# A mixture turned on the vector engine instead of on TensorE, in a transformer block on one Trainium2 core

## The chip, the cores and the metric

One Trainium2 chip, one core of it. The metric is the device time of one execution in microseconds (us); three executions of the kernel before were timed, and one more was profiled. All arrays are 32-bit floats.

## The reference: what is computed

A block for 256 tokens of width 2048: a norm modulated by a conditioning vector, one wide input product, two mixers (gated linear attention "gla", block attention "moba"), a gated mixture of their two up-projections, an output product with a residual, and a feed-forward part. What matters here is the mixture:

```python
y_gla = o_gla @ w_up_gla[l]
y_moba = o_moba @ w_up_moba[l]
g_gla, g_moba = jnp.split(jax.nn.sigmoid(gates), 2, axis=-1)
x = x + gt1[:, None] * ((g_gla * y_gla + g_moba * y_moba) @ w_out[l])
```

## The kernel before

TensorE (PE) multiplies in a reduced 32-bit format; for accuracy each operand is split into a high and a low half, and each product is three matmuls: high by high (L308), high by low weights (L309), low by high (L310). Two token groups m = 0, 1 of 128 tokens have a PSUM tile of 128 x 512 each.

Weights stream in tiles of 128 x 1024 (512 KB, two slices of the inner dimension), made by `w_tiles` (L113 on). SyncE (SP) issues the transfer into a buffer of the pool `rawp` (ten buffers), ScalarE (ACT) casts the high half `whi` (L124), VectorE (DVE) subtracts for the low half `wlo` (L125); these two have high priority and five buffers each (`hlp`). One tile feeds one step of twelve matmuls. So DVE can be up to some four tiles ahead of PE.

In the background a conditioning product runs beside this: its weights `araw` share `rawp`, and DVE accumulates them (L159, the first of a group L161); `background(per)` emits `per` such pieces a step. When a group is done, PE sums it across partitions (L184), ACT copies the row (L187), PE turns it (L190) and DVE adds three small results (L197 to L199).

The output of the mixture is needed with the model dimension on the partitions, for the product with `w_out`, while the up-projections deliver it with the tokens there. So it is turned. `up_moba(j)` forms one column block of 512 of the moba product and multiplies it by its gate (L647). `up_gla(j)` does so for the other branch (L653), adds both (L654), and `to_T` turns the sum: eight PE transposes of 128 x 128 (L638) into two PSUM tiles, then the high half by ACT (L243) and the low half by DVE (L244).

The order around it is: up_moba(0), up_moba(1), two gate products (blocks 16 and 17 of the input product, `in_block`), up_moba(2), up_gla(0), up_gla(1), up_gla(2), gate products 18 and 19, up_moba(3), up_gla(3), then `w_out` in column blocks (`block_tok` called for each). An up-projection has 4 tiles (48 matmuls), a gate product and a block of `w_out` 8. The programmer writes this order; a scheduler then places the instructions of each engine by priority, readiness and free buffers, and each engine runs its own list strictly in order.

Of the kernel before, what the change touches and what calls it, by code (L numbers as in the profile page):

```python
# [8 lines left out]
F32 = mybir.dt.float32  # L9
F32R = mybir.dt.float32r  # L10
# [4 lines left out]
ALU = mybir.AluOpType  # L15
AX = mybir.AxisListType

P = 128
# [3 lines left out]
W = 512  # L22
# [18 lines left out]
def block_kernel(ctx, tc, x, c, ada_w, ada_b, norm1_g, w_in, gate_w2, gate_b, gla_norm_g,  # L41
                 w_up_gla, w_up_moba, w_out, norm2_g, w_ffn_in, w_ffn_out, final_g, out):
    nc = tc.nc
# [7 lines left out]
    rawp = ctx.enter_context(tc.tile_pool(name="rawp", bufs=NRAW))  # L51
# [5 lines left out]
    def slot(name, dt=F32):  # L57
        return slots.tile([P, W], dt, name=name, tag="slot")

    def mm_ps():  # L60
        return mmp.tile([P, W], F32, name="mm", tag="mm")

    def ax_ps():
        return axp.tile([P, W], F32, name="ax", tag="ax")

    tt = nc.vector.tensor_tensor
# [8 lines left out]
    for j in (0, 2):  # L75
        for m in range(2):
            t = rawp.tile([P, 2, W], F32, name="x", tag="raw")
# [15 lines left out]
    for r0, v in ((0, ada_b[0, 0:2 * D]), (32, norm1_g[0]), (48, ada_b[0, 3 * D:5 * D]), (80, norm2_g[0]), (96, gate_b[0])):  # L93
        v = v.rearrange("(k p) -> k p", p=P)
# [19 lines left out]
    def w_tiles(w_ap, k0, k1, c0, ncols=W):  # L114

        wv = w_ap.rearrange("(k p) n -> p k n", p=P)
        step = 2 * W // ncols
        for k in range(k0, k1, step):
            n = min(step, k1 - k)
            raw, hi, lo = (pool.tile([P, 2 * W], dt, name=name, tag=tag)[:, 0:n * ncols] for pool, dt, name, tag in  # L120
                           ((rawp, F32, "raw", "raw"), (hlp, F32R, "whi", "hi"), (hlp, F32R, "wlo", "lo")))
            nc.sync.dma_start(raw.rearrange("p (k n) -> p k n", n=ncols), wv[:, k:k + n, c0:c0 + ncols])
            with tc.high_priority(offset=HP):
                nc.scalar.copy(hi, raw)  # L124
                tt(lo, raw, hi.bitcast(F32), ALU.subtract)  # L125
            yield k, [(hi[:, q * ncols:(q + 1) * ncols], lo[:, q * ncols:(q + 1) * ncols]) for q in range(n)]
# [98 lines left out]
    def background(n):  # L225
        owed[0] += n
        while owed[0] >= 1 and bg:
            owed[0] -= 1
            try:
                next(bg[0])  # L230
            except StopIteration:
                bg.pop(0)
                owed[0] += 1
        if not bg:
            owed[0] = 0.0
# [6 lines left out]
    def split_T(ps, hi, lo):  # L242
        nc.scalar.copy(hi, ps)  # L243
        tt(lo, ps, hi.bitcast(F32), ALU.subtract)  # L244
# [57 lines left out]
    def prod_tok(ps, m, hi, lo, wt, k0, first, last):  # L302

        for q, (wh, wl) in enumerate(wt):
            k = k0 + q
            xh, xl = kx(hi, k, m), kx(lo, k, m)
            f, l = first and q == 0, last and q == len(wt) - 1
            mm(ps, lhsT=xh, rhs=wh, start=f, stop=False)  # L308
            mm(ps, lhsT=xh, rhs=wl, start=False, stop=False)  # L309
            mm(ps, lhsT=xl, rhs=wh, start=False, stop=l)  # L310
# [10 lines left out]
    res = [[None, None] for _ in blocks]  # L321
# [286 lines left out]


    owed_T = []  # L610

    def block_tok(hi, lo, w_ap, nk, c0, per=0, ncols=W, lag=0):

        ps = [mm_ps(), mm_ps()]
        out = [t[:, 0:ncols] for t in ps]
        behind = []
        for k, g in w_tiles(w_ap, 0, nk, c0, ncols):
            behind.append((k, g))
            prod_tok(out[0], 0, hi, lo, g, k, k == 0, k + len(g) == nk)
            if len(behind) > lag:  # L620
                k1, g1 = behind.pop(0)
                prod_tok(out[1], 1, hi, lo, g1, k1, k1 == 0, k1 + len(g1) == nk)
            background(per)
            if owed_T and k > 0:
                to_T(*owed_T.pop())
        for k1, g1 in behind:
            prod_tok(out[1], 1, hi, lo, g1, k1, k1 == 0, k1 + len(g1) == nk)
        return out

    mx_h, mx_l = [None] * 8, [None] * 8  # L630

    def to_T(src, hi, lo, kp0):

        for i in range(2):
            ps = ax_ps()
            for q in range(2):
                for m in range(2):
                    nc.tensor.transpose(ps[:, q * T + m * P:q * T + (m + 1) * P],  # L638
                                        src[m][:, (2 * i + q) * P:(2 * i + q + 1) * P], ident)
            hi[kp0 + i], lo[kp0 + i] = slot("th", F32R), slot("tl", F32R)  # L640
            split_T(ps, hi[kp0 + i], lo[kp0 + i])

    def up_moba(j):
        ps = block_tok(om_h, om_l, w_up_moba, 8, j * W, pace[0])
        for m in range(2):
            g = res[13 + 2 * j][m]
            tt(g, ps[m], g, ALU.mult)  # L647

    def up_gla(j):
        ps = block_tok(og_h, og_l, w_up_gla, 8, j * W, pace[0])  # L650
        for m in range(2):
            g, y = res[12 + 2 * j][m], res[13 + 2 * j][m]
            tt(g, ps[m], g, ALU.mult)  # L653
            tt(g, g, y, ALU.add)  # L654
        to_T(res[12 + 2 * j], mx_h, mx_l, 2 * j)

    pace[0] = PACES[3]
    up_moba(0)
    up_moba(1)
    for bi in (16, 17):  # L660
        in_block(bi, 0, KT)()
    up_moba(2)
    up_gla(0)
    up_gla(1)
    up_gla(2)
    for bi in (18, 19):
        in_block(bi, 0, KT)()
# [62 lines left out]
    for j in range(4):  # L730
# [3 lines left out]
        if j < 3:  # L734
            ps = block_tok(mx_h, mx_l, w_out, KT, j * W, pace[0])
            while gt1[j] is None:
                background(1)
            for m in range(2):
                resid(m, j, 0, W, ps[m], gt1, j)
                for i in range(2):  # L740
                    norm2_T(j, i, m)
        else:
            while bg:
                background(1)
            preload_sqrt()
            ps = block_tok(mx_h, mx_l, w_out, KT, j * W, 0, 256)
            for m in range(2):
                resid(m, j, 0, 256, ps[m], gt1, 3)
                norm_part(m)
                norm2_T(j, 0, m)  # L750
            ps = block_tok(mx_h, mx_l, w_out, KT, j * W + 256, 0, 256, lag=KT)
            with tc.high_priority(offset=HP2):
                for m in range(2):
                    resid(m, j, 256, 256, ps[m], gt1, 4)
                    norm2_T(j, 1, m)
                    norm2_rstd(m)
                    if m == 0:
                        norm2(0, range(0, SPL))
                norm2(0, range(SPL, 8))
                norm2(1, range(8))  # L760
# [4 lines left out]
    for half, pairs in enumerate((range(0, 6), range(6, 11))):  # L765
        ac_h, ac_l = [None] * (2 * len(pairs)), [None] * (2 * len(pairs))
        for jj, j in enumerate(pairs):
# [4 lines left out]
            for m in range(2):  # L772
                t = slot("sa")
# [8 lines left out]
        if half == 1:  # L782
            for j in range(4):
                t = slot("fg")
# [4 lines left out]
        for j in range(4):  # L789
# [14 lines left out]
            with tc.high_priority(offset=HP2):  # L804
                for m in range(2):
# [3 lines left out]
                    for i in (2, 0, 1, 3):  # L809
                        t = x1[m][i]  # L810
# [32 lines left out]
```

## Time and profile before

| | us |
|---|---|
| median of three executions | 1460.25 |
| lowest, highest | 1459.01, 1460.31 |
| the profiled execution | 1460.44 |
| its span, first to last instruction | 1458.7 |
| PE busy in the span | 1434.1 |
| DVE busy | 1033.9 |
| ACT busy | 701.9 |

A row of the profile groups instructions by line, engine, operation and tiles, written out<-in. Matmuls overlap, so their durations add up to more than the busy time; the distance between starts tells what one costs. A wait is named after what ended last before the waiting instruction began. The granted clock is given as a share of the full one.

### The profile page before, as it was taken

How to read it: one execution, taken by the hardware profiler on the slowest of the kernel's cores; microseconds unless marked ns; L12 is line 12 of the kernel's file. 1: busy time of each engine (PE TensorE's matmuls, PEld its weight loads, DVE VectorE, ACT ScalarE, POOL GpSimd, SP SyncE). 2: the span in 40 equal slices, each digit the busy share in tenths (PEclk: the TensorE clock that was granted, in tenths of full speed). 3: DMA queues.
4: the chain of work that ended last, by engine and by line, in shares of the span. 5: the costliest groups of instructions: out<-in, count | busy, mean ns of one | idle time of the engine just before them, and what ended most of it. 6: DMA issues, size and time to landing. Idle time of an engine off the chain costs nothing.

```text
span 1458.7 us, 18395 instructions
## 1 busy us (share of the span) xinstructions
PE 1434.1 (98%) x6776; PEld 1178.4 (81%) x6776; DVE 1033.9 (71%) x1203; ACT 701.9 (48%) x936; POOL 8.6 (1%) x26
## 2 busy tenths in 40 slices
PE   6999999999999999999999999999999999999997
PEld 3788787888788878888888888888888888888887
DVE  4899988987799989888686676545555445555554
ACT  5745444644558534445654444444333444444443
POOL 0000000000000000000000000000000000000000
PEclk9999999999999999999999999999999999999999
DMA  9989999995636999999497888655566665556541
GB/s 333 362 305 367 337 323 308 316 317 184 199 114 205 371 335 336 328 324 369 147 322 267 268 282 288 193 182 188 195 194 192 197 188 188 188 187 224 189 150 59
DMA packets 191867, 365.49 MB, mean 251 GB/s; under 512 B 13848, under 2 KB 31484, under 8 KB 191776
## 3 DMA queue, kind: packets, MB, share of 16 engines
q1 hardware_dynamic: 189440, 360.56, 73.3%
q10 hardware_dynamic: 2336, 3.75, 0.8%
q8 instruction: 53, 0.87, 0.2%
q14 instruction: 38, 0.31, 0.1%
HBM read 362.16 MB, written 2.10 MB: 250 GB/s over the span
## 4 chain that ended last, share of the span: by engine, by line
PE 94%; DVE 2%; DMA 2%; ACT 1%; issue 1%; SPq 0%; DVEq 0%; ACTq 0%
PE mm L310 29%; PE mm L309 29%; PE mm L308 29%; DVE wlo L125 1%; DMA araw<-in_ada_w_dram 1%; PE ax L638 1%; PE ax L455 1%; DMA x<-in_x_dram 1%; DVE acc L159 0%; DMA w<-in_gla_gate_w_dram 0%; PE ax L184 0%; PE ax L276 0%; PE ax L690 0%; PE ax L334 0%; PE ax L153 0%
## 5 line engine op out<-in xcount | busy, mean ns | idle before, releaser
L125 DVE TENSOR_TENSOR wlo<-raw,whi 128x1024 fp32r<-128x1024 f32 x488 | 594.2, 1222 | 330.6 <-ACT whi L124 328.8
L124 ACT CAST whi<-raw 128x1024 fp32r<-128x1024 f32 x488 | 512.4, 1053 | 635.1 <-PE mm L310 367.2
L308 PE MATMUL mm<-whi,h2h 128*128 128x512 f32 x704 | 275.1, 391 | 1.0 <-ACT h2h L727 0.9
L310 PE MATMUL mm<-whi,h2l 128*128 128x512 f32 x704 | 274.2, 390 | 0.3 <-DVE h2l L728 0.3
L309 PE MATMUL mm<-wlo,h2h 128*128 128x512 f32 x704 | 274.0, 389 | 0.0
L309 PE MATMUL mm<-wlo,hTh 128*128 128x512 f32 x640 | 251.9, 394 | 0.4 <-DVE wlo L125 0.3
L308 PE MATMUL mm<-whi,hTh 128*128 128x512 f32 x640 | 250.3, 396 | 1.4 <-ACT hTh L296 1.3
L310 PE MATMUL mm<-whi,hTl 128*128 128x512 f32 x640 | 250.3, 393 | 0.5 <-DVE hTl L298 0.5
L159 DVE SCALAR_TENSOR_TENSOR acc<-araw,cs,acc 128x1024 f32<-128x1024 f32 (+1 forms) x184 | 227.4, 1236 | 26.7 <-DMA araw<-in_ada_w_dram 25.9
L308 PE MATMUL mm<-whi,th 128*128 128x512 f32 (+1 forms) x552 | 200.6, 363 | 0.0
L310 PE MATMUL mm<-whi,tl 128*128 128x512 f32 (+1 forms) x552 | 200.2, 363 | 0.0
L309 PE MATMUL mm<-wlo,th 128*128 128x512 f32 (+1 forms) x552 | 200.2, 363 | 0.0
L308 PEld LDWEIGHTS mm<-whi,h2h 128*128 128x128 f32 x704 | 132.2, 188 | 28.6 <-ACT h2h L727 1.7
L310 PEld LDWEIGHTS mm<-whi,h2l 128*128 128x128 f32 x704 | 132.2, 188 | 28.3 <-DVE h2l L728 0.7
L309 PEld LDWEIGHTS mm<-wlo,h2h 128*128 128x128 f32 x704 | 132.2, 188 | 27.2
L308 PEld LDWEIGHTS mm<-whi,hTh 128*128 128x128 f32 x640 | 120.7, 189 | 28.8 <-issue 2.2
L309 PEld LDWEIGHTS mm<-wlo,hTh 128*128 128x128 f32 x640 | 120.6, 188 | 27.3 <-DVE wlo L125 2.8
L310 PEld LDWEIGHTS mm<-whi,hTl 128*128 128x128 f32 x640 | 120.8, 189 | 25.5 <-DVE hTl L298 1.3
L310 PEld LDWEIGHTS mm<-whi,tl 128*128 128x128 f32 x552 | 104.3, 189 | 16.3 <-issue 0.4
L309 PEld LDWEIGHTS mm<-wlo,th 128*128 128x128 f32 x552 | 104.2, 189 | 16.0 <-issue 0.4
L308 PEld LDWEIGHTS mm<-whi,th 128*128 128x128 f32 x552 | 104.4, 189 | 15.8
L360 DVE TENSOR_TENSOR r<-mm,r 128x512 f32<-128x512 f32 x84 | 55.9, 684 | 13.5 <-PE mm L310 13.3
(205 smaller groups left out, 855.1 us busy)
## 6 DMA issues: line engine op xcount, KB each, us to landing
araw<-in_ada_w_dram SPq DMA_DIRECT2D x176, 512.0 KB, 5.6
raw<-in_w_ffn_in_dram SPq DMA_DIRECT2D x176, 512.0 KB, 3.5
raw<-in_w_in_dram SPq DMA_DIRECT2D x160, 512.0 KB, 5.7
raw<-in_w_ffn_out_dram SPq DMA_DIRECT2D x88, 512.0 KB, 3.6
raw<-in_w_out_dram SPq DMA_DIRECT2D x32, 512.0 KB, 6.5
araw<-in_ada_w_dram SPq DMA_DIRECT2D x32, 256.0 KB, 6.4
raw<-in_w_up_moba_dram SPq DMA_DIRECT2D x16, 512.0 KB, 5.2
raw<-in_w_up_gla_dram SPq DMA_DIRECT2D x16, 512.0 KB, 7.3
```

The lines of the kernel that those rows point to most:

```text
L124: nc.scalar.copy(hi, raw)
L125: tt(lo, raw, hi.bitcast(F32), ALU.subtract)
L159: stt(a, vq, cs[:, k:k + 1], a, ALU.mult, ALU.add)
L308: mm(ps, lhsT=xh, rhs=wh, start=f, stop=False)
L309: mm(ps, lhsT=xh, rhs=wl, start=False, stop=False)
L310: mm(ps, lhsT=xl, rhs=wh, start=False, stop=l)
L360: tt(res[bi][i], ps[i], res[bi][i], ALU.add)
L455: mm(ps[:, s], lhsT=e[:, s], rhs=e[:, s], start=True, stop=True)
L638: nc.tensor.transpose(ps[:, q * T + m * P:q * T + (m + 1) * P], src[m][:, (2 * i + q) * P:(2 * i + q + 1) * P], ident)
```

## The change

`up_gla` no longer calls `to_T`. It writes the sum of the two branches into one buffer of the pool of raw weights (`mixed`), and puts a generator, `square_T`, on a list. Each step of a following `block_tok` advances the generator by one piece. It turns the 128 x 1024 sum in sixteen DVE instructions, each of which takes 32 partitions by eight runs of 32 columns, turns each 32 x 32 square, and writes it to another group of 32 partitions of a second raw buffer (`turned`). Four pieces: eight turns, eight turns, and twice the high half (ACT, L660) and the low half (DVE, L661) of one of the two result tiles. Gate products (`in_block`) do not advance the list.

```diff
@@ block_tok @@
             if owed_T and k > 0:
                 to_T(*owed_T.pop())
+            if owed_sq and next(owed_sq[0], True):
+                owed_sq.pop(0)
@@ new @@
+    def square_T(src, hi, lo, kp0):
+        v = src.rearrange("p (b i) -> p b i", i=P)
+        turned = rawp.tile([P, 2 * W], F32, name="turned", tag="raw")
+        o = turned.rearrange("p (b i) -> p b i", i=P)
+        for a in range(0, P, 32):
+            for b in range(0, P, 32):
+                nc.vector.transpose(o[b:b + 32, :, a:a + 32], v[a:a + 32, :, b:b + 32])
+            if a % 64:
+                yield False
+        o = turned.rearrange("p (m k t) -> p k m t", m=2, k=4)
+        for i in range(2):
+            h, l = slot("th", F32R), slot("tl", F32R)
+            part = o[:, 2 * i:2 * i + 2]
+            nc.scalar.copy(h.rearrange("p (k m t) -> p k m t", k=2, m=2), part)
+            tt(l.rearrange("p (k m t) -> p k m t", k=2, m=2), part,
+               h.bitcast(F32).rearrange("p (k m t) -> p k m t", k=2, m=2), ALU.subtract)
+            hi[kp0 + i], lo[kp0 + i] = h, l
+            yield i == 1
@@ up_gla @@
+        mixed = rawp.tile([P, 2 * W], F32, name="mixed", tag="raw")
         for m in range(2):
             g, y = res[12 + 2 * j][m], res[13 + 2 * j][m]
             tt(g, ps[m], g, ALU.mult)
-            tt(g, g, y, ALU.add)
-        to_T(res[12 + 2 * j], mx_h, mx_l, 2 * j)
+            tt(mixed[:, m * W:(m + 1) * W], g, y, ALU.add)
+        owed_sq.append(square_T(mixed, mx_h, mx_l, 2 * j))
```

In the changed program L647 is L670, L653 is L677, L654 is L678, the turns are L653, and the halves L660 and L661.

The order in which DVE's instructions stand changes with it, at three places shown here. In the names, r12, r14 and r18 are the gla gates of the first, second and fourth mixture, r13, r15, r17 and r19 hold the other branch, mm is a product in PSUM, and wlo is the low half of a weight tile.

DVE from the last tile of up_gla(0) (wlo_4611) on, before; wlo_4653, 4688, 4709 and 4730 are the four tiles of up_gla(1):

```order
L125 TENSOR_TENSOR wlo_4611<-raw_4609,whi_4610 128x1024
L647 TENSOR_TENSOR r17_0_4455<-mm_4459,r17_0_4455 128x512
L647 TENSOR_TENSOR r17_1_4456<-mm_4460,r17_1_4456 128x512
L159 SCALAR_TENSOR_TENSOR acc_4682<-araw_4704,cs_106,acc_4682 128x1024
L125 TENSOR_TENSOR wlo_4653<-raw_4651,whi_4652 128x1024
L159 SCALAR_TENSOR_TENSOR acc_4682<-araw_4725,cs_106,acc_4682 128x1024
L125 TENSOR_TENSOR wlo_4688<-raw_4686,whi_4687 128x1024
L159 SCALAR_TENSOR_TENSOR acc_4682<-araw_4746,cs_106,acc_4682 128x1024
L125 TENSOR_TENSOR wlo_4709<-raw_4707,whi_4708 128x1024
L125 TENSOR_TENSOR wlo_4730<-raw_4728,whi_4729 128x1024
L653 TENSOR_TENSOR r12_0_322<-mm_4544,r12_0_322 128x512
L653 TENSOR_TENSOR r12_1_323<-mm_4545,r12_1_323 128x512
```

The same place in the changed program, where wlo_4636 is the first tile of up_gla(1):

```order
L125 TENSOR_TENSOR wlo_4611<-raw_4609,whi_4610 128x1024
L670 TENSOR_TENSOR r17_0_4455<-mm_4459,r17_0_4455 128x512
L670 TENSOR_TENSOR r17_1_4456<-mm_4460,r17_1_4456 128x512
L677 TENSOR_TENSOR r12_0_322<-mm_4544,r12_0_322 128x512
L678 TENSOR_TENSOR mixed_4627<-r12_0_322,r13_0_351 128x512
L677 TENSOR_TENSOR r12_1_323<-mm_4545,r12_1_323 128x512
L678 TENSOR_TENSOR mixed_4627<-r12_1_323,r13_1_352 128x512
L197 TENSOR_TENSOR G1_123<-ax_4659,scb_112 128x4
L199 TENSOR_TENSOR SH1_125<-ax_4659,vT_110 128x4
L198 TENSOR_TENSOR G1_123<-G1_123,vT_110 128x4
L653 STREAM_TRANSPOSE turned_4669<-mixed_4627 32x8x32 x7
L125 TENSOR_TENSOR wlo_4636<-raw_4634,whi_4635 128x1024
```

The instructions that read up_gla(0)'s product have moved ahead of all tiles of up_gla(1), and seven turns stand ahead of the first of them.

DVE at the end of up_gla(1) in the changed program; wlo_4734 is its last tile, wlo_4766 the first of up_gla(2). Before, all four tiles of up_gla(2) stood ahead of the instructions that read this product (L653), and one of gate product 18 between each two of them:

```order
L125 TENSOR_TENSOR wlo_4734<-raw_4732,whi_4733 128x1024
L661 TENSOR_TENSOR tl_4729<-turned_4669,th_4728 128x512
L159 SCALAR_TENSOR_TENSOR acc_4665<-araw_4750,cs_106,acc_4665 128x1024
L661 TENSOR_TENSOR tl_4754<-turned_4669,th_4753 128x512
L677 TENSOR_TENSOR r14_0_380<-mm_4632,r14_0_380 128x512
L677 TENSOR_TENSOR r14_1_381<-mm_4633,r14_1_381 128x512
L678 TENSOR_TENSOR mixed_4757<-r14_0_380,r15_0_409 128x512
L678 TENSOR_TENSOR mixed_4757<-r14_1_381,r15_1_410 128x512
L653 STREAM_TRANSPOSE turned_4782<-mixed_4757 32x8x32 x10
L125 TENSOR_TENSOR wlo_4766<-raw_4764,whi_4765 128x1024
```

Ten of the sixteen turns stand in one piece between the sum and the next product's first tile.

DVE at the end of up_gla(3) in the changed program; wlo_5402 is its last tile, wlo_5461 the first of `w_out`:

```order
L125 TENSOR_TENSOR wlo_5402<-raw_5400,whi_5401 128x1024
L159 SCALAR_TENSOR_TENSOR acc_5157<-araw_5418,cs_106,acc_5157 128x1024
L677 TENSOR_TENSOR r18_0_5039<-mm_5338,r18_0_5039 128x512
L678 TENSOR_TENSOR mixed_5421<-r18_0_5039,r19_0_5224 128x512
L677 TENSOR_TENSOR r18_1_5040<-mm_5339,r18_1_5040 128x512
L678 TENSOR_TENSOR mixed_5421<-r18_1_5040,r19_1_5225 128x512
L653 STREAM_TRANSPOSE turned_5480<-mixed_5421 32x8x32 x8
L125 TENSOR_TENSOR wlo_5461<-raw_5459,whi_5460 128x1024
L159 SCALAR_TENSOR_TENSOR acc_5157<-araw_5477,cs_106,acc_5157 128x1024
L653 STREAM_TRANSPOSE turned_5480<-mixed_5421 32x8x32 x2
L125 TENSOR_TENSOR wlo_5491<-raw_5489,whi_5490 128x1024
```

Before, four tiles of `w_out` stood ahead of the two L653 there; now none does, and eight turns come first.

## Rows read from the trace of the kernel before

**Rows 1.** The page, engines: busy us (share of the span) and instructions.

```profile
PE 1434.1 (98%) x6776; PEld 1178.4 (81%) x6776; DVE 1033.9 (71%) x1203; ACT 701.9 (48%) x936; POOL 8.6 (1%) x26
```

**Rows 2.** Busy time by stretch: length, each engine's us, then granted clock, DMA share, GB/s.

```profile
540.00:560.00 20.00, 20.00 (x95) 16.30 (x95) 19.88 (x23) 8.46 (x9) 0.00 (x0) 1.00 0.93 318
...
600.00:620.00 20.00, 20.00 (x90) 16.57 (x89) 17.91 (x17) 7.39 (x7) 0.00 (x0) 1.00 0.95 319
```

**Rows 3.** Waits of PE from 480 to 760 us: total, times, longest.

```profile
PE mm L308 <- ACT h2h L727: 0.9, 1, 0.9
PE mm L310 <- DVE h2l L728: 0.3, 1, 0.3
```

**Rows 4.** Timeline of PE, start and duration in us: up_gla(0), first and last matmuls.

```profile
516.28 0.39 PE L308 MATMUL mm<-whi,ogh 128*128 128x512 f32 x1
...
526.93 0.39 PE L310 MATMUL mm<-whi,ogl 128*128 128x512 f32 x1
```

**Rows 5.** Timeline of PE in up_gla(2): six transposes between matmuls.

```profile
547.46 0.39 PE L309 MATMUL mm<-wlo,ogh 128*128 128x512 f32 x1
547.69 0.82 PE L638 MATMUL ax<-ident,r 128*128 128x128 f32 x6
...
548.57 0.40 PE L308 MATMUL mm<-whi,ogh 128*128 128x512 f32 x1
```

**Rows 6.** Timeline of DVE from wlo_4611 on, idle time and its end in brackets.

```profile
514.85 1.23 DVE L125 TENSOR_TENSOR wlo<-raw,whi 128x1024 fp32r<-128x1024 f32 x1 [0.83 <-ACT whi L124]
515.99 1.28 DVE L647 TENSOR_TENSOR r<-mm,r 128x512 f32<-128x512 f32 x2
517.19 1.27 DVE L159 SCALAR_TENSOR_TENSOR acc<-araw,cs,acc 128x1024 f32<-128x1024 f32 x1
518.38 1.22 DVE L125 TENSOR_TENSOR wlo<-raw,whi 128x1024 fp32r<-128x1024 f32 x1
519.51 1.28 DVE L159 SCALAR_TENSOR_TENSOR acc<-araw,cs,acc 128x1024 f32<-128x1024 f32 x1
```

**Rows 7.** Groups of DVE, shapes apart: count, busy us, mean ns, idle before.

```profile
L723 DVE TENSOR_TENSOR x1g<-x1g,ax 128x256 f32<-128x256 f32 x16 | 6.1, 415 | 0.6 <-PE ax L717 0.6
...
L161 DVE TENSOR_SCALAR acc<-araw,cs 128x1024 f32<-128x1024 f32 x7 | 5.2, 747 | 0.0
```

**Rows 8.** Timeline of DVE: a dependent pair, and runs of one instruction without waits.

```profile
691.74 0.68 DVE L680 TENSOR_TENSOR tmp<-mm,gate 128x512 f32<-128x512 f32 x1
692.46 0.69 DVE L681 TENSOR_TENSOR x<-tmp,x 128x512 f32<-128x512 f32 x1
...
718.10 1.08 DVE L723 TENSOR_TENSOR x1g<-x1g,ax 128x256 f32<-128x256 f32 x3
...
720.69 1.40 DVE L728 SCALAR_TENSOR_TENSOR h2l<-x1g,SH,h2h 128x128 fp32r<-128x128 f32 x5
```

**Rows 9.** A background group's end: PE timeline, then ACT's group.

```profile
531.57 0.63 PE L184 MATMUL ax<-acc,ones 128*32 128x256 f32 x6
...
L187 ACT COPY rowsum<-ax 128x256 f32<-128x256 f32 x4 | 1.5, 373 | 0.0
```

**Rows 10.** Early in the kernel: stretches as in rows 2, then PE's timeline.

```profile
26.00:27.00 1.00, 0.49 (x2) 0.45 (x3) 0.91 (x2) 1.00 (x3) 0.00 (x0) 1.00 1.07 367
...
28.00:29.00 1.00, 1.00 (x3) 0.81 (x4) 0.65 (x2) 0.95 (x1) 0.00 (x0) 0.51 1.10 356
...
30.00:31.00 1.00, 1.00 (x3) 0.78 (x3) 1.00 (x2) 0.60 (x1) 0.00 (x0) 0.50 1.06 375
31.00:32.00 1.00, 1.00 (x5) 0.76 (x4) 0.70 (x2) 0.33 (x1) 0.00 (x0) 0.78 1.10 351
...
28.50 0.63 PE L308 MATMUL mm<-whi,hTh 128*128 128x512 f32 x1
28.93 0.63 PE L309 MATMUL mm<-wlo,hTh 128*128 128x512 f32 x1
```

**Rows 11.** DMA issues of w_up_gla: count, KB each, median us to landing.

```profile
raw<-in_w_up_gla_dram SPq DMA_DIRECT2D x16, 512.0 KB, 7.3
```

More of the change, by code (lines that the diff above doesn't have):

```diff
@@ L610, in block_kernel @@
     owed_T = []
+    owed_sq = []
     def block_tok(hi, lo, w_ap, nk, c0, per=0, ncols=W, lag=0):
```

## The prediction

> **What bounds the kernel now.** I read the engine totals first: TensorE (PE) is busy 98% of the span and VectorE (DVE) 71% [rows 1]. An average hides where the change lands, so next the stretches in which the four mixtures are made and turned (516 to 632 us). There PE is busy all the time at full clock, DVE 90 to 99% (17.9 and 19.9 of 20), and the transfers 93 to 95% [rows 2]. The waits of PE from 480 to 760 us come to 1.2 us, both from the later norm stage [rows 3]: here PE waits for nobody. So PE's own instructions set the time, one matmul every 0.227 us: up_gla(0) starts at 516.28, its 48th and last matmul at 526.93, 10.65 us for 47 intervals [rows 4]. A weight tile costs PE one step of 12 matmuls, 2.72 us.
>
> PE waits for nobody because DVE is far ahead. DVE starts the low half of the last tile of up_gla(0) (wlo_4611, just ahead of the two L647) at 514.85 us [rows 6]; PE starts that product's first tile at 516.28 [rows 4] and needs the fourth three steps later, near 524.4. That lead, nearly four steps, is the cover under which DVE's waits for PE (L647, L653) cost nothing.
>
> **What is removed.** 32 PE transposes (8 a mixture). From the start of the L309 at 547.46 to that of the L308 at 548.57 run this L309, six transposes and one L310: 1.11 us, less 2 x 0.227, is 0.66 for six, 0.11 each [rows 5]. 32 x 0.11 = **3.5 us off PE**, all of it on the path. The high and low halves of the turned tiles (L243, L244) remain as L660 and L661, with SBUF in place of PSUM as the source: taken as equal, 0.6 us on DVE for each of eight.
>
> **What is added.** 64 DVE transposes of 32 partitions x 8 x 32, so 256 elements a lane. No row shows one. The same 256 elements in 128 lanes take 0.415 us alone [rows 7] and follow each other every 0.33 us: three in 1.08, (1.08 - 0.415) / 2 [rows 8]. Bounds: below, 128 elements a lane, five in 1.40, 0.28 each [rows 8]; above, 512 elements every 0.60 us, as the two L647 are spaced (1.28 us together, one 0.68) [rows 6, 8], should filling and emptying the squares cost twice. I take 0.42, the nearest row's own duration with nothing overlapped. In the trace instructions of this kind overlap by some 0.08 us [rows 7, 8]; all of them start at partition 0. The Trainium skill (VectorE: DVE Perf Modes, "Two Vector instructions with no wait between them") says that an instruction whose input or output starts in another group of 32 partitions than the last one's is held until everything earlier has finished, and most turns here change group; by it the overlap is lost and the sum below stands, while with the overlap kept (0.33) it would be about 4 us smaller. No row here shows a change of group.
>
> 64 x 0.42 is 27 us of DVE work. The idle share of rows 2 alone would nearly hold that, spread out. The order decides.
>
> **What is moved, and the cost.** The order of DVE changes more than the diff says. Before, wlo of all four tiles of up_gla(1) stand ahead of the L653 that wait for the end of up_gla(0). Now L677 and L678 come first, then seven turns, and only then wlo_4636, the first tile of up_gla(1). DVE stops at L677 until PE has ended up_gla(0), and PE cannot go on until DVE has made wlo_4636: the lead is spent waiting, then PE waits. The same stands at the ends of up_gla(1) (ten turns ahead of wlo_4766) and up_gla(3) (eight ahead of wlo_5461, the first tile of w_out), and without turns at the end of up_gla(2).
>
> Prices: wlo 1.22 us alone, 1.13 to the next start [rows 6]; L159 1.20 [rows 6]; a 128x512 add 0.60 to the next [rows 6], 0.72 if the next needs its result [rows 8]; L161 0.75 [rows 7]. Take E as the end of a product's last matmul, its start + 0.39 (527.32 at the first) [rows 4]; unhindered, PE would start the next at E - 0.16, and L309, the first that needs wlo, two L308 later at E + 0.3.
> - End of up_gla(0): L677 of the second half starts at E, L678 at 0.72. Three tiny adds (L197 to L199) wait for PE's L184 (0.63), ACT's row copy (0.37) [rows 9] and two L190, and end near 1.65. Seven turns: 4.6. wlo: 5.8. PE itself has about 1.1 us of L184, L190 and L308 meanwhile. Lost: **4.7**.
> - End of up_gla(1): DVE comes 0.4 late; L677 0.4, L678 1.0 and 1.6, done 2.35, ten turns 6.55, wlo 7.8. PE could have gone on at 0.3. Lost: **7.5**.
> - End of up_gla(2): L677 0.36, L678 1.08, wlo from 1.7 to 2.9. Lost: **2.6**.
> - End of up_gla(3): L677 0, L678 0.72, turns from 1.44, eight to 4.8, wlo 6.0. Lost: **5.7**.
>
> Together 20.5 us, 25 turns among them. Without a lead, every step in which DVE needs more than 2.72 us shows too. In up_gla(1): L161 + 4 turns + wlo 3.56, L159 + 3 turns + wlo 3.59, L159 + 2 turns + wlo 3.17: 2.2 over. In up_gla(2) the first step (one turn, wlo: 1.55) is under and the next two over: 0.8. After up_gla(2) the lead grows again through block 18, but in block 19 three tiny adds now stand ahead of wlo_5184 and wait for PE's L190 in the step before it. So the lead is gone when the 16 turns of the third mixture come: up to the first tile of up_gla(3) 6 wlo, 5 L159, 16 turns and one L661 take 20.1 us against six steps of 16.3, with some 0.6 in hand: 3.2. In w_out's first steps 3.17 and 3.59: 1.3. Together 7.5.
>
> The clock: from about 28.0 to 31.4 us the granted clock is 0.50, the lower level of 1.2 GHz, after a stretch in which PE stood for about half of the time; matmuls are then 0.43 us apart [rows 10], which loses 3.4 x (1 - 0.227/0.43) = 1.6 us. The stops of 7.5 and 5.7 us are longer than any in rows 3 and I expect that after each; but a slow PE hides the 0.8 and 1.3 of overruns behind them. Net 1.1.
>
> Costed at nothing: the two raw buffers that mixed and turned hold out of ten. The transfer that comes out tightest is the first tile of block 18, issued when wlo_4766 is done (7.8 after the end of up_gla(1)) and needed at the end of up_gla(2), 7.5 + 10.9 = 18.4 after it; with 7.3 us to landing [rows 11] 3 us are over. If that cover fails, the price is the excess per tile.
>
> **Sum.** 20.5 + 7.5 + 1.1 - 3.5 = +25.6 us on the profiled execution's 1460.4 us (0.2 over the median of the three runs): **1486.0 us**, 1.8% slower. With turns at 0.28 the four waits (25 turns) are 17, the overruns (some 30 turns, not all showing) 2.5, less 3.5: +16, 1476. At 0.60: 25 and 14, less 3.5: +36, 1496.
>
> **Rivals.**
> 1. *Cover holds: faster.* If DVE still ran ahead, so that the turns fell into its idle tenth, only the 3.5 us would show: 1456.9. For it: the idle share in rows 2, and that no product needs the mixture at once. It decides at the end of up_gla(0): it holds if wlo_4636 is done within 1.1 us of E. Against it: engines take instructions in order, and the two additions alone need longer. 0.04. Gains and losses that cancel: 0.03.
> 2. *Cheap turns.* At 0.28 to 0.36 us the overruns shrink to half and less: 1476 to 1481. For it: overlapping neighbours in rows 8. 0.25.
> 3. *Dear turns.* At 0.55 us or more, some 50 turns on the path add 7 us and up: 1493 to 1500. For it: each square must be filled before it is emptied, and no row has such an access. 0.15.
> 4. *Transfers become the bound.* The queue is busy 93 to 95% [rows 2]; while DVE holds buffers nothing is issued. Were 6 us of it not made up, 1492. Against it: PE stands at the same time. 0.08.
>
> My forecast, turns near 0.42 (1481 to 1492), has 0.45. The range holds it and most of the second, third and fourth: 1474 to 1500. Slower by over 0.2% (about what a measurement of this kernel can tell from no change; 2.9 us): 0.93; within 0.2%: 0.03; faster by more: 0.04.
>
> **What would show it.** In the changed profile: PE waiting for DVE's wlo at L309, three times 4 to 8 us and once 2 to 3; DVE idle up to 9 us ahead of L677, with PE as the releaser; turns of 0.3 to 0.5 us; the granted clock at 0.5 for some 3 us behind the longest stop; L638 without its 32. A PE without waits from 520 to 640 us, or waits on ACT or on transfers in place of DVE, would show the argument wrong; turns of another length would leave its form and move its size.

## The result and the profile after

| | us |
|---|---|
| before, median of 4 runs on the same chip | 1459.82 |
| after, median of 4 runs (1490.20 to 1492.54) | 1492.05 |
| ratio after / before, 95% interval | 1.0219, 1.0203 to 1.0235 |
| forecast, range | 1486.0, 1474 to 1500 |

The change makes the kernel 2.2% slower; the profiled execution after has a span of 1490.2 us against 1458.7. The engine totals hardly tell it: PE 1434.1 us before [rows 1], 6 us more now with 32 instructions fewer, and DVE 28 us more.

```profile
PE 1440.1 (97%) x6744; PEld 1178.9 (79%) x6744; DVE 1061.8 (71%) x1267; ACT 698.1 (47%) x936; POOL 8.6 (1%) x26
```

The waits of PE tell it. Before, PE waited 1.2 us from 480 to 760 us, none of it for weights [rows 3]. After, from 500 to 720 us:

```profile
PE mm L309 <- DVE wlo L125: 22.2, 9, 7.5
PE mm L308 <- ACT whi L124: 0.5, 1, 0.5
PE ax L190 <- ACT rowsum L187: 0.5, 1, 0.5
```

Nine waits for the low half of a weight tile (total, times, longest). The four long ones stand at the ends of up_gla(0) to up_gla(3); PE's timeline, with the idle time and its end in brackets:

```profile
533.85 0.79 PE L309 MATMUL mm<-wlo,ogh 128*128 128x512 f32 x1 [3.50 <-DVE wlo L125]
...
555.34 0.79 PE L309 MATMUL mm<-wlo,ogh 128*128 128x512 f32 x1 [7.54 <-DVE wlo L125]
...
570.88 0.50 PE L309 MATMUL mm<-wlo,hTh 128*128 128x512 f32 x1 [2.19 <-DVE wlo L125]
...
648.54 0.80 PE L309 MATMUL mm<-wlo,th 128*128 128x512 f32 x1 [5.92 <-DVE wlo L125]
```

DVE's timeline at the end of up_gla(0) answers to [rows 6]. Where DVE ran on to the halves of the next product without a gap, DVE now stands 8.73 us until PE has ended the product, forms the mixture, turns seven strips, and only then makes the half for which PE waits:

```profile
526.28 0.69 DVE L677 TENSOR_TENSOR r<-mm,r 128x512 f32<-128x512 f32 x1 [8.73 <-PE mm L310]
...
528.37 0.69 DVE L678 TENSOR_TENSOR mixed<-r,r 128x512 f32<-128x512 f32 x1
...
529.42 3.12 DVE L653 STREAM_TRANSPOSE turned<-mixed 32x256 f32<-32x256 f32 x7
532.57 1.23 DVE L125 TENSOR_TENSOR wlo<-raw,whi 128x1024 fp32r<-128x1024 f32 x1
```

The group of the turns (count, busy us, mean ns, idle before): one lasts 436 ns, and seven in 3.12 us start every (3.12 - 0.436) / 6 = 0.447 us, so nothing overlaps.

```profile
L653 DVE STREAM_TRANSPOSE turned<-mixed 32x256 f32<-32x256 f32 x64 | 27.9, 436 | 1.2
```

ACT's list changed in the same way, which the prediction does not tell. Before, ACT casts a high half every 2.72 us while up_gla(0) runs (from 516.48 us on). After, it casts none there: it stands 13.14 us until the row copy (L187) can start behind PE's L184, and then casts the four halves of up_gla(1) in one go:

```profile
528.24 0.37 ACT L187 COPY rowsum<-ax 128x256 f32<-128x256 f32 x1 [13.14 <-PE ax L184]
528.51 3.88 ACT L124 CAST whi<-raw 128x1024 fp32r<-128x1024 f32 x4
```

Their weights were not what was missing. The transfers of these four tiles were issued from 502.79 to 513.66 us, with 6.1 us to landing as the median in this run. SP's next transfer of w_up_gla, for up_gla(2), comes only at 534.49: SP waits 17.6 us for DVE's L161, which reads a buffer that SP is to fill again (SP's timeline):

```profile
513.66 0.37 SPq L122 DMA_DIRECT2D raw<-in_w_up_gla_dram  x1
516.38 0.37 SPq L147 DMA_DIRECT2D araw<-in_ada_w_dram  x1
534.49 4.63 SPq L122 DMA_DIRECT2D raw<-in_w_up_gla_dram  x2
```

So at this stop the halves were late by the order in the lists of ACT and DVE, not by the transfers.

Busy time by stretch, with columns as in [rows 2]. In the first stretch DVE works 5.11 of 14 us and the transfers run at 0.18; then DVE is full. The last three are single microseconds from the three places where the granted clock is at 0.50:

```profile
516.00:530.00 14.00, 13.00 (x64) 9.93 (x62) 5.11 (x12) 1.76 (x3) 0.00 (x0) 1.00 0.18 60
530.00:540.00 10.00, 6.50 (x17) 4.83 (x16) 9.74 (x17) 2.39 (x3) 0.00 (x0) 0.66 0.18 55
540.00:560.00 20.00, 12.46 (x45) 9.62 (x44) 19.55 (x31) 4.09 (x5) 0.00 (x0) 0.74 0.64 198
...
533.00:534.00 1.00, 0.15 (x1) 0.15 (x1) 1.00 (x2) 0.00 (x0) 0.00 (x0) 0.50 0.00 0
550.00:551.00 1.00, 0.00 (x0) 0.00 (x0) 0.97 (x3) 0.00 (x0) 0.00 (x0) 0.50 1.02 397
646.00:647.00 1.00, 0.00 (x0) 0.00 (x0) 0.97 (x3) 0.00 (x0) 0.00 (x0) 0.50 0.12 47
```

The starts of the products (their first matmuls on PE's timeline, before and after) place the loss; the forecast's terms are put to the same stretches, each less its share of the saved transposes (16 in the first, 8 in the second, 8 in w_out):

| from the start of | before, us | after, us | lost up to the next row | forecast |
|---|---|---|---|---|
| up_gla(0) | 516.28 | 516.56 | 15.1 | 13.4 |
| block 18 | 552.66 | 568.07 | 2.6 | 1.7 |
| up_moba(3) | 598.18 | 616.22 | 4.0 | 3.2 |
| w_out | 619.94 | 642.00 | 9.2 | 6.1 |
| the product after w_out | 715.94 | 747.20 | 0.2 | 0 |

The forecast had 1.1 us for the clock besides.

### The profile page after: what moved, and what is told of

Read it like the earlier page. It is cut to its first block, busy times and chain, and to the rows that moved or that the text cites. A ratio compares the mean times of both kernels' runs of the same rounds, so it can differ in the third digit from the quotient of the medians.

```text
span 1490.2 us, 18382 instructions
## 1 busy us (share of the span) xinstructions
PE 1440.1 (97%) x6744; PEld 1178.9 (79%) x6744; DVE 1061.8 (71%) x1267; ACT 698.1 (47%) x936; POOL 8.6 (1%) x26
## 4 chain that ended last, share of the span: by engine, by line
PE 90%; DVE 6%; issue 2%; DMA 2%; ACT 1%; SPq 0%; DVEq 0%; ACTq 0%
PE mm L309 28%; PE mm L310 28%; PE mm L308 28%; DVE wlo L125 1%; DVE turned L653 1%; DVE acc L159 1%; DMA araw<-in_ada_w_dram 1%; PE ax L455 1%; PE ax L641 1%; PE ax L184 0%; DMA rows<-in_gla_gate_b_dram 0%; PE ax L276 0%; DMA cT<-in_c_dram 0%; PE ax L334 0%; DVE r L677 0%
## 5 line engine op out<-in xcount | busy, mean ns | idle before, releaser
L308 PE MATMUL mm<-whi,h2h 128*128 128x512 f32 x704 | 275.1, 391 | 1.0 <-ACT h2h L751 0.9
L309 PE MATMUL mm<-wlo,h2h 128*128 128x512 f32 x704 | 274.0, 389 | 0.0
L309 PE MATMUL mm<-wlo,hTh 128*128 128x512 f32 x640 | 252.1, 394 | 2.7 <-DVE wlo L125 2.5
L308 PE MATMUL mm<-whi,hTh 128*128 128x512 f32 x640 | 249.2, 396 | 1.4 <-ACT hTh L296 1.3
L309 PE MATMUL mm<-wlo,th 128*128 128x512 f32 (+1 forms) x552 | 201.2, 364 | 6.1 <-DVE wlo L125 6.1
L308 PE MATMUL mm<-whi,th 128*128 128x512 f32 (+1 forms) x552 | 199.7, 364 | 0.0
L308 PEld LDWEIGHTS mm<-whi,h2h 128*128 128x128 f32 x704 | 132.2, 188 | 28.6 <-ACT h2h L751 1.7
L309 PEld LDWEIGHTS mm<-wlo,h2h 128*128 128x128 f32 x704 | 132.2, 188 | 27.3
L309 PEld LDWEIGHTS mm<-wlo,hTh 128*128 128x128 f32 x640 | 120.6, 188 | 30.7 <-DVE wlo L125 6.3
L308 PEld LDWEIGHTS mm<-whi,hTh 128*128 128x128 f32 x640 | 120.6, 188 | 28.7 <-issue 2.2
L309 PEld LDWEIGHTS mm<-wlo,th 128*128 128x128 f32 x552 | 104.7, 190 | 23.3 <-DVE wlo L125 7.2
L308 PEld LDWEIGHTS mm<-whi,th 128*128 128x128 f32 x552 | 104.4, 189 | 16.0
L360 DVE TENSOR_TENSOR r<-mm,r 128x512 f32<-128x512 f32 x84 | 55.9, 685 | 13.4 <-PE mm L310 13.3
```

The costliest lines, as they stand in the source:

```text
L360: tt(res[bi][i], ps[i], res[bi][i], ALU.add)
```

## The experiments

The question was what the loss is made of. My theory: the order (the sums and turns stand ahead of the next product's halves on DVE, because `mixed` is drawn from the ring of prefetched weight tiles). Rivals: the amount (28 us of turns cost wherever they stand), the transfers (two ring buffers fewer), the clock.

### The ring buffer alone, without turns on DVE

The sum goes into `mixed` as in the change, but PE turns it:

```diff
-        owed_sq.append(square_T(mixed, mx_h, mx_l, 2 * j))
+        to_T([mixed[:, 0:W], mixed[:, W:]], mx_h, mx_l, 2 * j)
```

> The sum of the two branches goes into a buffer of the ring of prefetched weights, as in the changed kernel, but the matrix engine turns it, as before: no turn on the vector engine, its amount of work as before. Theory of the order (the ring buffer of the sum lets the four multiplications and additions come ahead of the next product's weight halves, so each product begins with its halves still to be made): the four waits for halves stay, each shorter by the turns that stood in them (3.1, 4.5, none and 3.6 us of 3.5, 7.5, 2.2 and 5.9); with the small stops and refills some 9 to 10 us, about 1469 us, between 1465 and 1473. Theory of the amount (the 28 us of turns are the cost wherever they stand): 1458 to 1461 us, no wait for halves at the ends. Theory of the clock: no drop without long stops, so no more than the waits themselves.

Measured: 1485.61 us, ratio 1.0174 (1.0159 to 1.0189). Not one turn on DVE, and 25 us are lost against 32 in the change. DVE's timeline has the same gap ahead of the first L677:

```profile
525.92 0.69 DVE L677 TENSOR_TENSOR r<-mm,r 128x512 f32<-128x512 f32 x1 [8.73 <-PE mm L310]
```

and on PE's timeline what stood behind the turns is another chain, from the sum over PE's own transposes and ACT's halves:

```profile
527.49 0.41 PE L641 MATMUL ax<-ident,mixed 128*128 128x128 f32 x2 [0.24 <-DVE mixed L678]
...
528.76 0.87 PE L641 MATMUL ax<-ident,mixed 128*128 128x128 f32 x6 [0.29 <-DVE mixed L678]
531.41 1.22 PE L308 MATMUL mm<-whi,ogh 128*128 128x512 f32 x2 [1.78 <-ACT whi L124]
```

The amount falls as the main cause. My number was some 17 us too low: I took the turns out of the waits and kept the rest, but each stop is a whole chain, and here PE's transposes stand in it, which the kernel before places inside the next product. The expectation on the clock failed too. No wait of PE in this stretch is longer than 1.8 us, yet the granted clock is at 0.50 at four places, some 17 us of PE's work together, about 8 of the 25 us by the factor of the forecast. Ahead of the first of them PE was busy for 1.85 of 4.16 us (527.25 to 531.41), at full clock.

### A copy in place of the turns

```diff
-            for b in range(0, P, 32):
-                nc.vector.transpose(o[b:b + 32, :, a:a + 32], v[a:a + 32, :, b:b + 32])
+            if a == 0:
+                nc.vector.tensor_copy(turned, src)
```

> The sixteen turns of a mixture are replaced by one copy of 128x1024 on the vector engine, at the place of the first turns: the squares are not turned, so the result differs; everything else of the change stays (ring buffers, halves from the vector and scalar engines, no transposes on the matrix engine). Theory of the order: as the run with the sum in the ring, less 3.5 us for the transposes that are gone, and 0.7 to 1.3 us more for the copy in each of three waits: 1465 to 1472 us. Theory of the amount: 4 copies instead of 28 us of turns, 1456 to 1460 us.

This kernel leaves the turning out, so its output is not the mixture. Measured: 1482.75 us, ratio 1.0154 (1.0137 to 1.0171): 22 us lost with 4 copies of 0.69 us. Again more than expected, and again the chain filled up: ACT now has a half of the mixture ahead of the weight halves, and PE waits mostly for whi instead of wlo:

```profile
530.16 0.75 PE L308 MATMUL mm<-whi,ogh 128*128 128x512 f32 x2 [2.65 <-ACT whi L124]
...
549.05 1.22 PE L308 MATMUL mm<-whi,ogh 128*128 128x512 f32 x2 [4.03 <-ACT whi L124]
```

In both runs the edit also moved rows on ACT or PE, so they show that a loss of this size needs no turns, not what each link costs.

### The turns behind the first halves

```diff
-            if owed_sq and next(owed_sq[0], True):
+            if owed_sq and k > 0 and next(owed_sq[0], True):
```

> The changed kernel with the turns begun one step later in the next product, so that on the vector engine the four multiplications and sums still stand ahead of the next product's first weight halves, but no turn does at the first of them. Theory of the order, as in the prediction (turns in front of the first halves are 3.1, 4.5 and 3.6 us of the waits): 1492 less some 11, so 1478 to 1484 us. Theory that the held ring buffers alone set the wait (the sums, then a chain by the scalar engine to the first halves, whatever stands between, as the runs without turns still lost 22 and 25 us): 1486 to 1493 us.

Measured: 1495.22 us, ratio 1.0233 (1.0217 to 1.0248). No gain: it lies above the ranges of both theories. PE's waits from 500 to 760 us:

```profile
PE mm L309 <- DVE wlo L125: 18.5, 11, 4.4
PE mm L308 <- ACT whi L124: 2.8, 2, 2.3
```

The longest wait fell from 7.5 to 4.4 us, and there are more of them. Together they are 21.3 us against 22.7 in the change (wlo and whi), while PE worked at the low clock for about 20 us against 14. DVE is busy for 19.6 to 19.8 of each 20 us from 540 to 580 us, so a turn moved out of one wait has no idle time to go to and falls into the next.

### The turns without the ring

The sum in place, its turned form in two small tiles of 128x512, so 32 turns of 32x128 a mixture (the halves are then made in pieces of 128x256):

```diff
-        mixed = rawp.tile([P, 2 * W], F32, name="mixed", tag="raw")
...
-            tt(mixed[:, m * W:(m + 1) * W], g, y, ALU.add)
+            tt(g, g, y, ALU.add)
...
-        turned = rawp.tile([P, 2 * W], F32, name="turned", tag="raw")
+        turned = [slot("turned") for _ in range(2)]
```

> All turns stay on the vector engine, but no buffer of the ring of weights is taken: the sum is formed in place as before, and its turned form goes into two buffers of 128x512 of the pool of small tiles, so each turn is 32x128 and there are 32 of them per mixture instead of 16. On the vector engine four halves of the next product's weights now come ahead of the multiplication and sum, as before the change. Theory of the order: the waits at the ends of up_gla(0) and up_gla(1) are under 1 us each; what is left is lack of room, as between the two runs with a ring of 8 (1484.4 less 1473.8, so some 11 us), more if a 32x128 turn takes more than half of 0.436 us (32 x 0.25 is 8 us a mixture): 1466 to 1476 us. Theory that the turns cost by their amount wherever they stand: 1485 us or more.

Measured: 1472.78 us, ratio 1.0078 (1.0061 to 1.0095). All the turns are there, 128 of them with more DVE time than in the change (32.5 us busy against 27.9), and 19 of the 32 us are back. DVE's timeline at the end of up_gla(0): a half of the next product between the product and the sum, and eight turns at a time between halves.

```profile
526.80 1.28 DVE L679 TENSOR_TENSOR r<-mm,r 128x512 f32<-128x512 f32 x2
528.00 0.68 DVE L680 TENSOR_TENSOR r<-r,r 128x512 f32<-128x512 f32 x1
528.60 1.22 DVE L125 TENSOR_TENSOR wlo<-raw,whi 128x1024 fp32r<-128x1024 f32 x1
...
532.94 2.01 DVE L654 STREAM_TRANSPOSE turned<-r 32x128 f32<-32x128 f32 x8
534.98 1.23 DVE L125 TENSOR_TENSOR wlo<-raw,whi 128x1024 fp32r<-128x1024 f32 x1
```

Block 18 starts at 549.90 us, 2.8 before the kernel before and 18.2 before the change: over three products the turns cost nothing. Then the lead is used up. PE stops in blocks 18 and 19 (7.0 us over before, from 549.90 to 602.41) and in w_out (7.8, from 624.30 to 728.07). That is the amount: DVE is full and PE is not. About 5 of these 14.8 us are the clock, at 0.50 again for some 11 us of PE's work behind the waits.

```profile
550.00:580.00 30.00, 30.00 (x133) 24.35 (x131) 28.85 (x55) 9.94 (x14) 0.00 (x0) 1.00 0.66 196
580.00:600.00 20.00, 16.28 (x62) 11.96 (x61) 19.25 (x20) 7.26 (x8) 0.00 (x0) 0.83 1.02 371
```

### A pool of their own, and its control

`mixed` and `turned` in a pool of two buffers, with `NRAW = 8` to make room:

```diff
-NRAW = 10
+NRAW = 8
+    sqp = ctx.enter_context(tc.tile_pool(name="sqp", bufs=2))
```

> The sum and its turned form get a pool of two buffers of their own, taken from the ring of weights, which has 8 instead of 10 throughout. All turns stay. Now the weight halves of the next products can be placed ahead of the sums. Theory of the order: the waits at the ends of the products shrink to under 2 us each; what is left is the vector engine's lack of room (28 us of turns, of which 21 fall between 516 and 640 us, against some 16 us of idle time there before): some 1465 to 1478 us, plus what 8 buffers cost by themselves (next run). Theory of the amount: 1485 us or more, as the changed kernel.

> The kernel before with 8 instead of 10 buffers in the ring of weights, nothing else: what the two buffers that the change takes from the ring cost by themselves, and the control of the run with a pool of its own. Theory of the order: within 5 us of before (1458 to 1465). Theory of the transfers (the ring two buffers shorter starves the weights): 1475 us or more.

Measured: 1484.44 us with the pool (ratio 1.0168, 1.0152 to 1.0183), 1473.75 for the kernel before with a ring of 8 (1.0093, 1.0078 to 1.0108). I had the control wrong: two buffers fewer cost 13.3 us, but 11.9 of them ahead of up_gla(0) (its start is at 528.13 against 516.28), where the change keeps all ten. From there to the product after `w_out` the control takes 199.78 us and the kernel before 199.66, so the two buffers that the change holds are, as mere room for transfers, not the cause of its loss. Against its control the pool costs 10.7 us, as the run without the ring does against before (11.6). Its time alone does not tell the two theories apart; its first three products (up_gla(0) to up_gla(2)) do: 33.67 us with all turns in place, 33.68 in the run without the ring, 36.38 before, 51.51 in the change.

### Two mixtures only

```diff
-        owed_sq.append(square_T(res[12 + 2 * j], mx_h, mx_l, 2 * j))
+        if j < 2:
+            owed_sq.append(square_T(res[12 + 2 * j], mx_h, mx_l, 2 * j))
+        else:
+            to_T(res[12 + 2 * j], mx_h, mx_l, 2 * j)
```

> As the run with the turns in small tiles, but only for the mixtures of up_gla(0) and up_gla(1); the matrix engine turns the last two as before. Theory of room: in that run the stop of blocks 18 and 19 (7.0 us over before) came after the turns of the first two mixtures had used up the lead of the vector engine, so it stays, and the 7.8 us lost in w_out go with the last two mixtures; 16 transposes saved are 1.8 us: 1464 to 1468 us. Theory that each mixture costs its own share (15 us over four): half, 1465 less 1.8 and less: 1459 to 1464 us. No cost at all for two mixtures: 1458 to 1460 us.

Measured: 1466.31 us, ratio 1.0039 (1.0026 to 1.0052), in the range of the theory of room. w_out loses 0.6 us; the stop in block 18 stays, now as one wait of PE's own transposes of the third mixture for a sum that DVE reaches late:

```profile
573.36 0.69 PE L641 MATMUL ax<-ident,r 128*128 128x128 f32 x2 [4.76 <-DVE r L680]
```

### Turn all squares at once, and let GpSimd move them

```diff
+        for m in range(2):
+            nc.vector.transpose(sq[m], src[m])
...
-                    nc.vector.transpose(o[m][b:b + 32, :, a:a + 32], v[m][a:a + 32, :, b:b + 32])
+                    nc.gpsimd.tensor_copy(o[m][32 * b:32 * b + 32, :, a:a + 32], v[m][a:a + 32, :, b])
```

> No ring buffer, and the vector engine turns all squares of a 128x512 half in place of partitions by one instruction (2 per mixture instead of 16 or 32); the idle GpSimd engine then moves the squares between the groups of partitions, 32 copies of 32x128 per mixture. If the order and the room on the vector engine are all that costs, with some 6 us of added work on it instead of 28 the transposes saved on the matrix engine remain: 1456 to 1462 us. Rival: GpSimd's copies are slow (over 1 us each, so 32 us a mixture) or slow the vector engine's own work, so the halves for w_out come late: 1465 to 1490 us.

Measured: 1483.62 us, ratio 1.0151 (1.0136 to 1.0166): the rival, though the copies are not slow one by one. Up to block 18 it is as good as the run without the ring (550.12 us); then ACT stands at halves that wait for GpSimd, with weight halves queued behind them (PE's waits):

```profile
PE mm L308 <- ACT th L666: 9.8, 1, 9.8
PE mm L308 <- ACT whi L124: 5.3, 1, 5.3
```

The next two kernels leave the last mixture to PE and give the halves more time, two steps and then four; all owed mixtures advance at each step:

```diff
-            if a % 64:
-                yield False
+            yield False
+        for _ in range(4):
+            yield False
...
-            if owed_sq and next(owed_sq[0], True):
-                owed_sq.pop(0)
+            owed_sq[:] = [q for q in owed_sq if not next(q, True)]
```

> The vector engine turns squares in place of partitions (2 instructions per mixture) and GpSimd moves them, for the mixtures 0 to 2 only, with each mixture's halves two steps of a product later than before and all owed mixtures advanced at each step; the matrix engine turns the last mixture as in the kernel before. In the run with squares and moves the scalar engine stood at a half that waited for GpSimd (32 copies of 0.407 us are 13 us a mixture, longer than a product of 10.7 us) and the weight halves behind it came late, 5.3 us in block 18 and 9.8 us in w_out; with the time between them these two stops go. Theory of order and room: 24 transposes saved at 0.11 us are 2.6 us, 1457 to 1460 us. Rival: the copies are still not done where the scalar engine comes to the halves, or slow the vector engine: 1463 to 1472 us.

Measured with two steps: 1466.88 us, ratio 1.0040 (1.0027 to 1.0054). 3.3 us were gained by the start of w_out (616.69), and more than that lost there (10.7 in the profiled execution): DVE stood at a half of the third mixture, and then came late with the fourth sum, which PE turns (DVE's, then PE's timeline).

```profile
611.09 0.76 DVE L667 TENSOR_TENSOR tl<-turned,th 128x256 fp32r<-128x256 f32 x2 [6.71 <-ACT th L666]
...
627.97 0.66 PE L640 MATMUL ax<-ident,r 128*128 128x128 f32 x2 [7.34 <-DVE r L682]
```

> As the run before with moves by GpSimd for the mixtures 0 to 2, with the halves of each mixture two more steps later (four instead of two), so that those of mixture 2 are made in w_out, whose third weight tile is the first to need them. In the run before, 3.3 us were gained by the start of w_out (616.69 against 619.94 us), and 9.6 us were lost in w_out, where the vector engine had stood 6.7 us at a half of mixture 2 that waited for GpSimd and then came late with the sum that the matrix engine turns (7.3 us of wait). If that was all, this keeps the 3.3 us: 1456 to 1459 us. Rival: the halves of mixture 2 now come late for w_out's third weight tile, 11 us after its start: 1460 to 1466 us.

Measured with four steps: **1458.17 us, ratio 0.9984 (0.9975 to 0.9993)**, faster than the change by 34 us, and than the kernel before by 2.1 (1460.30 beside it), a gain at the edge of what can be told. PE's waits from 500 to 760 us are near those of [rows 3]:

```profile
PE ax L640 <- DVE r L682: 1.0, 1, 1.0
PE mm L308 <- ACT h2h L758: 0.9, 1, 0.9
PE mm L310 <- DVE h2l L759: 0.3, 1, 0.3
```

and its turns cost DVE 4.1 us for three mixtures where the change spends 20.9:

```profile
L650 DVE STREAM_TRANSPOSE sq<-r 128x512 f32<-128x512 f32 x6 | 4.1, 694 | 0.0
```

## Why the prediction was right, and where it was not

The measured 1492.05 us is inside the range, at the upper end of the band that had the largest chance (1481 to 1492), 6 us over 1486.0. It is also, by luck, the time of the fourth rival (1492); that rival's sign, PE waiting for transfers, is not there.

- *Direction, place and form: right.* DVE stands for PE at L677 (8.73 us, forecast up to 9), then PE for DVE at L309. Without the ring up_gla(0) to up_gla(2) are free of loss, with all the turns in place. That ACT's halves stand behind the stop too was not in the prediction; in the change it costs 0.5 us (L308), in the two runs without turns it is the largest wait.
- *The four waits: right.* Forecast 4.7, 7.5, 2.6 and 5.7 us. The rows show 3.50 with 0.5 and 0.5 ahead of it, 7.54, 2.19 and 5.92. A stop costs a little more than its wait: at the third, where the clock stayed up, the next matmul starts 2.47 us later than at the usual distance (571.22 in place of 568.75).
- *The turn: right.* 0.42 taken, 0.436 measured, 0.447 from start to start. The Trainium skill (VectorE: DVE Perf Modes, "Two Vector instructions with no wait between them") says that an instruction whose input or output starts in another group of 32 partitions than the one before is held until everything earlier has finished. The traces agree: where strips change their group, nothing overlapped, while neighbours in [rows 7, 8] did by 0.08. The run without the ring shows both side by side, as its turns go in pairs between the same two groups: the second of a pair starts 0.235 us after the first, which lasts 0.30, and the first of the next pair only 0.01 after the last has ended, so eight take 2.01 us.
- *The clock: mis-sized, the largest single part of the 6 us that were missing, at most 3.3 of them.* "I expect that after each" of the two longest stops, 3.4 us each, net 1.1. It fell three times, also at the stop of 3.5 us but not at that of 2.19, and PE's matmuls were 0.43 us apart for about 5.6, 4.6 and 3.5 us. By the forecast's factor (1 - 0.227/0.43) that is 6.5 us in place of 3.2, part of it hiding overruns as forecast.
- *w_out: mis-sized.* 9.2 against 6.1: a drop of the clock (1.7) and 1.6 us of waits for the later norm (L714), which the kernel before does not have. Why they appear is not shown by a run.
- *What the turns themselves cost: the step that failed.* The sum booked 25 turns at 0.42 in the four waits and read from it that a turn of 0.28 us would give 1476. No run has such a turn, but the reckoning behind it failed three times: with no turn at all and the same ring buffer it gave about 1469 and came to 1485.61, and to 1482.75 with a copy (forecast 1465 to 1472); with the turns behind the first halves it gave 1478 to 1484 and came to 1495.22. What the waits of the first two runs hold in place of the turns is the rest of the chain, ACT's halves above all; the clock comes on top in all three. The lead that is spent waiting is the larger cause: it costs 25 us without any turn, and taking it away saves 19. The turns' amount is the smaller: 11.6 us net without the ring, 15 with the 3.5 us that they save. (The two overlap: 25.1 and 11.6 are 36.7, and the change loses 32.2.) The amount is paid in blocks 18 and 19 and in w_out. The prediction's "DVE 90 to 99%" is read from the two stretches of [rows 2]; from 516 to 640 us DVE is busy 108.6 of 124 us, so 15.4 us idle, which is still too little for the 21 us of turns that fall there.
- *The first rival, that the cover holds,* came true for three products once the order let it. *The transfers* were rightly costed at nothing in this stretch, as SP's timeline and the control show.

Open: that `mixed` in the ring brings the sums to the front is shown by the two runs that keep all turns and take it out of the ring, and by the two that keep it there without turns. Why the scheduler does so is argued only; no run changed the scheduler itself.

## What to carry to other kernels

With the sum in the ring that also holds prefetched weights, the halves of the tiles behind it were no longer made ahead of it, on two engines, though the tiles themselves had been loaded (seen at up_gla(1)). Look for the pool of a new tile before costing its instructions, and price a lost lead as a chain to its end, not by the instruction in its middle. And turn the squares in place rather than in strips: a strip of 32 partitions and 256 columns took 0.436 us, all 128 partitions and 512 columns in place 0.694. Moving the squares by an engine with time, far enough ahead of who needs them, cost this kernel nothing.

## What was not expected of the hardware

A turn in place of 128x512 took 0.69 us, two a mixture, 1.4 us; the same squares in 16 strips of 32x256 took 7.15 us (16 x 0.447), moves included.

GpSimd's copies of 32x128 took longer the busier DVE was. In the first run with moves, 32 of them took 13.15 us while DVE was busy 5.41 of 13.20 us; in the last, 64 took 52.94 us, 0.83 each, with DVE busy 49.84 of 53.00:

```profile
534.03 13.15 POOL L657 COPY turned<-sq 32x128 f32<-32x128 f32 x32 [114.81 <-PE mm L310]
```

```profile
534.84 52.94 POOL L656 COPY turned<-sq 32x128 f32<-32x128 f32 x64 [114.74 <-PE mm L310]
```

The third mixture says the same: 32 copies took 12.66 us with two steps, where DVE was busy 5.90 of 12.70 us, and 25.57 with four, where it was busy 25.49 of 25.60. In the long stretch of the last run DVE's halves (wlo) took 1.291 us in place of 1.222. The Trainium skill (Advanced Engine Details and Errata, "Mode Summary") says that VectorE's second port is shared with GpSimd, so that GpSimd's instructions and VectorE's two-port ones block each other. The rows agree in that the two slow each other, and here GpSimd paid most of it; which of VectorE's instructions here use two ports, no run shows.
